# Weight pieces that begin with the kind the last one ended with, and low parts three pieces ahead, in a two-layer hybrid decoder trunk

## The chip, the cores and the metric

One core of one Trainium2 chip runs the whole computation. The metric is the device time of one execution in microseconds; a run's time is that of the slowest core, and here there is one. Engines are named as the profile names them: PE is TensorE (PEld its weight loads), DVE VectorE, ACT ScalarE, POOL GpSimd, SP SyncE, whose queue issues the weight loads.

## The reference

Two layers act on x, 256 positions by 2048 features, in float32. Cut to what matters:

```python
for l in range(DEPTH):
    h = rmsnorm(x, norm_mix_g[l])
    z = h @ w_in[l]                 # q | k | v | u | gates, 6656 columns
    y_attn = sliding_window_attention(q, k, v, q_norm_g[l], k_norm_g[l], attn_sinks[l])
    y_ssm = gelu(s5_ssm(u, ...))    # a diagonal complex state, scanned over the positions
    y_ssm = y_ssm * sigmoid(y_ssm @ ssm_glu_w[l] + ssm_glu_b[l])
    merged = g_attn * (y_attn @ w_attn_branch[l]) + g_ssm * (y_ssm @ w_ssm_branch[l])
    x = x + merged @ w_out[l]
    h2 = rmsnorm(x, norm_ffn_g[l])
    gu = h2 @ w_ffn_in[l]
    x = x + (silu(gu[..., :D_FF]) * gu[..., D_FF:]) @ w_ffn_out[l]
```

Nearly all arithmetic is in the products with weights.

## The kernel before

**Products in parts.** The activations and the weights are each split into a high part, rounded to TensorE's fp32r type, and a low part, what the rounding left. A product is high x high + low activation x high weight + high activation x low weight. The activations of one k tile (128 features) stand as [high | low], 2 x 256 columns, so a high weight tile takes one matmul of 512 columns and a low weight tile one of 256.

**Pieces.** Weights come in pieces of up to 4 k tiles by 256 output features, 512 KB each, some 880 in all, in one planned order (`want`, line 207, and the loops behind it). A slab of 256 output features takes 4 pieces where k is 2048, 2 where it is 1024 and 3 or 4 in the feed-forward output. Class `Weights` (lines 50 to 133) carries a piece through three steps, with 4 buffers each for raw pieces, high parts and low parts. `load` issues the DMA on SP's queue, `high` casts the raw piece to its high part on ScalarE (line 106), and `low` subtracts that from the raw piece on VectorE (line 121), into the low part. `low(n)` calls `high(n)` first. TensorE's loop calls `get(i)` for each piece, and `get` asks ahead:

```python
def get(self, i):
    self.high(i + 3)
    self.low(i + 2)
    self.load(i + 2 + self.LOADS)
    return self.ready.pop(i)
```

**The product loop.** `products` (line 274) takes each piece's 8 matmuls with high weights and then its 8 with low weights (lines 285 to 295: 4 k tiles, 2 tiles of 128 features), into one accumulator of two PSUM banks, of which there are 2 (`acc`). Low weights add into the second half of each bank. A few pieces aren't "wide": the first slab of the first layer takes three matmuls of 256 columns per tile, in one mixed order (line 303); so does the very last slab (line 323). The pair of slabs at line 1028 takes its pieces in turns.

**The order of everything else.** Each engine works through its instructions in the order in which the program issues them (`manual_schedule`, line 171). After each piece's matmuls `ck.tick()` (line 305) issues the jobs that are due at that piece: evictions of the slab before, a scan step, a stage of attention. `later(n, f)` sets a job n ticks ahead, `stages` runs a generator's stages one tick after the other, and `at` counts ticks from the layer's start. Jobs of a tick go in the order in which they were asked for. So the issue order is `get(i)`, matmuls of piece i, jobs of tick i, `get(i+1)`, and so on.

**A layer's order.** u, k, v and q projections; the attention gate (ga) projections; attention's output projection (ab); the SSM gate (gs) projections; GLU; the SSM's output projection (sb); the product with w_out; then the feed-forward stage in three parts, gate and up slabs (fg, fu) and output slabs (fo). Beside these:

- The scan (lines 759 to 769) is spread over the ticks up to number 110 of the layer, one or two steps a tick: products at line 766 and additions at 769, all on VectorE. Behind its last step `channels` (line 947) has its output matmuls (ys, line 963).
- Attention (lines 832 to 888) has eight head pairs, `attend(j)`, four ticks apart, the last a tick less. In one stage ScalarE takes the exponentials (line 862), VectorE adds the denominators and takes the reciprocal (lines 864 and 865), and ScalarE scales four score tiles with it (line 869); two ticks later TensorE transposes them (line 876), and a tick on makes the output y, which `split` turns into high and low parts of `ya`.
- `normed` (line 799) scales q and k: squares on ScalarE, sums on TensorE (line 806), logarithm and exponential on ScalarE (lines 369 and 370), the rest on VectorE (373 to 375).
- `evict_gs` (line 941) is issued one tick behind its slab: ScalarE copies half of the accumulator, VectorE adds the other (line 344) and multiplies by the norm (943), ScalarE takes two sigmoids (363).
- `evict_u` (line 717) has a multiplication on VectorE (719) and eight small copies, four on ScalarE (731) and four on VectorE (729).
- `coefficients` (line 562) runs on VectorE in slices of five steps a tick at the first layer's start.

Of the kernel before, what the change touches and what calls it, by code (L numbers as in the profile page):

```python
# [49 lines left out]
class Weights:  # L50
# [76 lines left out]
            self.n_low += 1  # L127

    def get(self, i):
        self.high(i + 3)  # L130
        self.low(i + 2)
        self.load(i + 2 + self.LOADS)
        return self.ready.pop(i)


# [32 lines left out]
def build(ctx, tc, a, out):  # L168
    nc = tc.nc
    v, s, g, pe = nc.vector, nc.scalar, nc.gpsimd, nc.tensor  # L170
# [12 lines left out]
    def nm(x):  # L183
        uid[0] += 1
        return f"{x}_{uid[0]}"
# [80 lines left out]
    for k, base in ((0, 0), (1, -P), (2, 0)):  # L266
# [4 lines left out]
        else:  # L271
            g.affine_select(out=nd, in_=nd, compare_op=ALU.is_gt, fill=MASKED, base=0, pattern=[[1, P]], channel_multiplier=-1)

    def products(key, rhs, wide):


        ps = accp.tile([P, 2, 512], F32, name=nm("acc"), tag="acc", bufs=2)
        pieces = plan[key]
        k = 0
        for i in pieces:  # L280
            hi, lo, m = W.get(i)
            last = i == pieces[-1]
            if wide:

                for lo_part in range(2):
                    for j in range(m):
                        x = rhs(k + j)
                        for t in range(2):
                            f = slice(t * P, t * P + P)
                            if lo_part:  # L290
                                o, w, r = ps[:, t, T:], lo[:, j, f], x[:, 0, :]
                            else:
                                o, w, r = ps[:, t, :], hi[:, j, f], x.rearrange("p a t -> p (a t)")
                            start = k + j == 0 and not lo_part
                            pe.matmul(o, w, r, start=start, stop=last and j == m - 1 and lo_part == 1, skip_group_check=True)  # L295
            else:
                for j in range(m):
                    x = rhs(k + j)
                    for t in range(2):
                        wh, wl = (w[:, j, t * P : t * P + P] for w in (hi, lo))  # L300
                        for n, (w, r) in enumerate(((wh, 0), (wh, 1), (wl, 0))):
                            start, stop = k + j + n == 0, last and j == m - 1 and n == 2
                            pe.matmul(ps[:, t, :T], w, x[:, r, :], start=start, stop=stop, skip_group_check=True)
            k += m
            ck.tick()
            yield ps

    def slab(key, rhs, wide):
        for ps in products(key, rhs, wide):
            pass  # L310
        return ps
# [14 lines left out]
    def pair(keys, rhs, wide, evict):  # L326

        gens = [products(key, rhs, wide) for key in keys]
        for _ in plan[keys[0]][:-1]:
            for gen in gens:  # L330
                next(gen)
        for i, gen in enumerate(gens):
            evict(i, next(gen))
# [43 lines left out]
    class Norm:  # L377
# [42 lines left out]
        def rhs(self, k):  # L420
            return self.h[:, k, :, :]
# [760 lines left out]
```

## Time and profile before

| | |
|---|---|
| median of 3 runs | 2632.5 us (2630.88 to 2633.15) |
| profiled execution, its own time | 2632.42 us |
| its span, first to last instruction | 2630.5 us |
| mean granted TensorE clock | 0.994 |
| instructions | 40564 |
| TensorE busy | 99% of the span |
| VectorE busy | 73% |
| ScalarE busy | 48% |
| HBM read, mean over the span | 471 MB, 181 GB/s with what is written |

The profile gives, for one execution, the busy time of each engine, groups of instructions by line, waits (who waited for whom, as inferred from semaphores) and the chain of work that ended last. In a timeline row stand the start in us, the time from the first start to the last end, the engine, the line, the operation, output tiles <- input tiles, the shape and the count of like instructions merged; a bracket shows idle time of the engine before it and what ended it. A row `x8` of matmuls spans eight that overlap each other, so the distance of starts is the better measure of their pace. Rows cut by the edge of a query's window count only what lies in it.

### The profile page before, as it was taken

The page shows a single profiled execution, that of the slowest core. Times are in us where ns is not written, and L with a number is a line of the kernel's source. Part 1 is how long each engine was busy: PE and PEld are TensorE (multiplying, and loading weights), DVE is VectorE, ACT ScalarE, POOL GpSimd, SP SyncE. Part 2 cuts the span into 40 slices and gives each one's busy share as a digit, 9 for nine tenths or more (in the row PEclk, how much of TensorE's full clock was granted, in tenths as well). Part 3 has the DMA queues.
Part 4 walks back from the last instruction along what each step waited for, and adds up shares of the span by engine and source line. Part 5 has one row for each costly group of instructions (what it writes and reads, how often), then busy time and mean ns, then how long its engine had stood idle before and what let it go on. Part 6 is the DMA issues. An engine that isn't in the chain of part 4 may idle for free.

```text
span 2630.5 us, 40564 instructions
## 1 busy us (share of the span) xinstructions
PE 2591.1 (99%) x15716; PEld 2259.7 (86%) x15716; DVE 1932.4 (73%) x3648; ACT 1267.8 (48%) x1725; POOL 29.0 (1%) x34
## 2 busy tenths in 40 slices
PE   7999899999999999999999999999999999999999
PEld 6878788888888888888888788888888888888888
DVE  8889997866765666566677999887666656665664
ACT  5666545544443444334455675465544434443442
POOL 2000000000000000000000000000000000000000
PEclk9999999999999999999999999999999999999999
DMA  6544455666655565566664445556656556655655
GB/s 203 169 129 144 145 170 164 200 209 194 203 172 191 190 189 179 192 199 187 199 201 160 141 149 170 178 173 211 213 185 187 183 199 188 190 186 187 188 180 172
DMA packets 139825, 477.85 MB, mean 182 GB/s; under 512 B 14960, under 2 KB 25456, under 8 KB 139632
## 3 DMA queue, kind: packets, MB, share of 16 engines
q1 hardware_dynamic: 139488, 475.06, 56.4%
q8 instruction: 123, 2.02, 0.3%
q14 instruction: 70, 0.57, 0.1%
q10 hardware_dynamic: 144, 0.20, 0.0%
HBM read 471.01 MB, written 4.19 MB: 181 GB/s over the span
## 4 chain that ended last, share of the span: by engine, by line
PE 81%; DVE 14%; ACT 3%; issue 1%; DMA 0%; SPq 0%; ACTq 0%; DVEq 0%
PE acc L295 79%; DVE wlo L121 5%; DVE S L769 3%; DVE sc L766 2%; ACT whi L106 1%; DVE wh L344 1%; DVE scs L855 1%; PE v L746 1%; PE ys L963 1%; ACT scs L869 1%; DVE ga L896 0%; DVE ga L916 0%; DMA w<-in_w_in 0%; PE acc L323 0%; PE bt L672 0%
## 5 line engine op out<-in xcount | busy, mean ns | idle before, releaser
L106 ACT CAST whi<-w 128x1024 fp32r<-128x1024 f32 (+1 forms) x881 | 910.6, 1047 | 769.6 <-PE acc L295 606.4
L121 DVE TENSOR_TENSOR wlo<-w,whi 128x1024 fp32r<-128x1024 f32 (+1 forms) x881 | 1061.4, 1219 | 221.2 <-ACT whi L106 220.2
L295 PE MATMUL acc<-h,whi 128*128 128x512 f32 x4448 | 1128.6, 396 | 0.8 <-DVE wh L344 0.8
L295 PEld LDWEIGHTS acc<-h,whi 128*128 128x128 f32 x4448 | 802.3, 189 | 156.8 <-issue 9.4
L295 PEld LDWEIGHTS acc<-h,wlo 128*128 128x128 f32 x4448 | 606.1, 190 | 53.5 <-DVE wlo L121 10.9
L295 PE MATMUL acc<-h,wlo 128*128 128x256 f32 x4448 | 621.8, 283 | 5.3 <-DVE wlo L121 5.3
L295 PE MATMUL acc<-hid,whi 128*128 128x512 f32 x1384 | 346.6, 392 | 0.0
L295 PEld LDWEIGHTS acc<-hid,whi 128*128 128x128 f32 x1384 | 248.9, 189 | 44.5
L337 DVE TENSOR_REDUCE j<-acc 128x512 f32<-128x1024 f32 x88 | 107.8, 1225 | 134.4 <-PE acc L295 134.4
L295 PEld LDWEIGHTS acc<-hid,wlo 128*128 128x128 f32 x1384 | 188.8, 190 | 13.5
L295 PE MATMUL acc<-hid,wlo 128*128 128x256 f32 x1384 | 193.0, 282 | 0.0
L1102 DVE TENSOR_TENSOR xn<-xn,acc 128x512 f32<-128x512 f32 x47 | 32.3, 688 | 173.5 <-PE acc L295 173.5
L769 DVE TENSOR_TENSOR S<-S,sc 128x32 f32<-128x32 f32 x1016 | 153.5, 222 | 0.0
L295 PE MATMUL acc<-mg,whi 128*128 128x512 f32 x512 | 128.2, 392 | 0.0
L766 DVE TENSOR_TENSOR sc<-scan_c,S 128x64 f32<-128x64 f32 x508 | 115.6, 269 | 0.0
L295 PEld LDWEIGHTS acc<-mg,whi 128*128 128x128 f32 x512 | 92.1, 189 | 16.5
L295 PE MATMUL acc<-yg,whi 128*128 128x512 f32 x384 | 96.2, 392 | 0.0
L295 PEld LDWEIGHTS acc<-yg,whi 128*128 128x128 f32 x384 | 69.1, 189 | 12.3
L295 PE MATMUL acc<-ya,whi 128*128 128x512 f32 x256 | 68.5, 410 | 10.0 <-DVE ya L161 6.0
L295 PEld LDWEIGHTS acc<-mg,wlo 128*128 128x128 f32 x512 | 69.8, 190 | 5.0
L351 ACT CAST hid<-j 128x512 fp32r<-128x512 f32 x44 | 27.4, 623 | 96.9 <-DVE j L1072 96.9
L295 PE MATMUL acc<-mg,wlo 128*128 128x256 f32 x512 | 71.4, 282 | 0.0
(238 smaller groups left out, 1500.7 us busy)
## 6 DMA issues: line engine op xcount, KB each, us to landing
w<-in_w_fi SPq DMA_DIRECT2D x352, 512.0 KB, 4.3
w<-in_w_in SPq DMA_DIRECT2D x207, 512.0 KB, 3.7
w<-in_w_fo SPq DMA_DIRECT2D x176, 512.0 KB, 4.4
w<-in_w_out SPq DMA_DIRECT2D x64, 512.0 KB, 4.4
w<-in_w_ab SPq DMA_DIRECT2D x32, 512.0 KB, 3.5
w<-in_w_sb SPq DMA_DIRECT2D x32, 512.0 KB, 4.1
w<-in_w_glu SPq DMA_DIRECT2D x16, 512.0 KB, 3.8
x<-in_x SPq DMA_DIRECT2D x8, 256.0 KB, 5.8
```

Source lines behind the costliest of these rows:

```text
L106: self.nc.scalar.copy(part[0][:, f, :], w[:, f, :])
L121: self.nc.vector.tensor_sub(lo[:, f, :], w[:, f, :], hi[:, f, :].bitcast(F32))
L295: pe.matmul(o, w, r, start=start, stop=last and j == m - 1 and lo_part == 1, skip_group_check=True)
L337: v.tensor_reduce(t, ps.rearrange("p s (a t) -> p s t a", a=2), axis=AX.X, op=ALU.add)
L344: v.tensor_add(t, t, ps[:, :, :T])
L351: s.copy(hi, src)
L746: pe.matmul(pss[r][:, c0 : c0 + P], bt[ri][o : o + 64, 2 * q4 + i, :], ur[o : o + 64, 2 * q4 + i, :], start=True, stop=True)
L766: v.tensor_mul(pr, scan_c[:, l, :, :, f], S[:, :, f, c - 1].unsqueeze(1).to_broadcast([P, 2, 2, 16]))
L769: v.tensor_add(S[:, :, f, c], S[:, :, f, c], pr[:, :, r, :])
L855: v.tensor_tensor_reduce(scs[b][:, f, :], scs[b][:, f, :], pv[:, f, :], 1.0, sk[:, b : b + 1], ALU.add, ALU.max, accum_out=mx[:, b, n : n ...
L869: s.activation(z, z, AF.Copy, scale=rd[:, b, n : n + 1])
L1102: v.tensor_add(t, t, ps[:, :, :T])
```

## The change

`get` asks for low parts three pieces ahead, with their casts, and for loads seven ahead of the piece in place of six. In `products` one flag, `at_low`, is kept over all pieces: a piece begins with the kind of weights that the flag names, and the flag is turned between its halves. The first matmul of a slab has the start flag whichever kind it is, the last the stop flag. Behind a piece that isn't wide the flag names low weights.

```diff
     def get(self, i):
-        self.high(i + 3)
-        self.low(i + 2)
-        self.load(i + 2 + self.LOADS)
+        self.low(i + 3)
+        self.load(i + 3 + self.LOADS)
         return self.ready.pop(i)
...
+    at_low = [False]
+
     def products(key, rhs, wide):
...
-                for lo_part in range(2):
+                for half in range(2):
+                    if half:
+                        at_low[0] = not at_low[0]
+                    lo_part = at_low[0]
                     for j in range(m):
                         x = rhs(k + j)
                         for t in range(2):
...
-                            start = k + j == 0 and not lo_part
-                            pe.matmul(o, w, r, start=start, stop=last and j == m - 1 and lo_part == 1, skip_group_check=True)
+                            start = k + j + half == 0
+                            pe.matmul(o, w, r, start=start, stop=last and j == m - 1 and half == 1, skip_group_check=True)
             else:
+                at_low[0] = True
                 for j in range(m):
```

## Rows read from the trace of the kernel before

**Rows 1.** The page's head and its busy times by engine.

```profile
span 2630.5 us, 40564 instructions
...
PE 2591.1 (99%) x15716; PEld 2259.7 (86%) x15716; DVE 1932.4 (73%) x3648; ACT 1267.8 (48%) x1725; POOL 29.0 (1%) x34
```

**Rows 2.** The chain that ended last, by line: 427 to 1370 us, then 290 to 400.

```profile
by line: PE acc L295 99.3%; PE bt L672 0.4%; PE ms L417 0.2%; PE k L683 0.1%
...
by line: DVE wlo L121 34.6%; DVE S L769 22.6%; DVE sc L766 17.8%; DVE ga L916 5.0%; ACT whi L106 4.6%; DVE wh L344 4.4%; DMA w<-in_w_in 3.1%; DVE gs L943 2.5%; DVE gs L344 2.2%; issue 2.1%; PE ys L963 0.6%; ACT gs L363 0.5%; ACTq L106 0.1%;
```

**Rows 3.** Busy time by stretch: bounds and length in us, then each engine, clock, DMA.

```profile
157.00:290.00 133.00, 125.49 (x760) 103.40 (x759) 128.54 (x534) 86.87 (x200) 3.63 (x2) 0.96 0.44 137
290.00:400.00 110.00, 103.33 (x590) 87.57 (x588) 109.35 (x433) 51.90 (x70) 0.00 (x0) 1.00 0.52 164
1440.00:1590.00 150.00, 145.39 (x895) 121.66 (x894) 145.78 (x558) 99.33 (x214) 3.63 (x2) 0.99 0.47 148
...
427.00:1370.00 943.00, 943.00 (x5534) 830.37 (x5533) 641.75 (x696) 430.58 (x503) 4.47 (x3) 1.00 0.60 193
1745.00:2630.00 885.00, 881.91 (x5074) 776.83 (x5072) 573.21 (x598) 375.37 (x411) 0.00 (x0) 1.00 0.59 190
```

**Rows 4.** Waits of VectorE, 157 to 290 us: total us, times, longest.

```profile
DVE wlo L121 <- ACT whi L106: 0.8, 2, 0.6
```

**Rows 5.** Waits of TensorE over the whole span: total us, times, longest.

```profile
PE acc L295 <- DVE ya L161: 6.0, 2, 3.8
...
PE ys L963 <- DVE S L769: 2.1, 1, 2.1
```

**Rows 6.** Timeline of TensorE in the feed-forward stage; the last two from narrower windows.

```profile
1005.84 2.00 PE L295 MATMUL acc<-h,whi 128*128 128x512 f32 x8
1007.68 1.11 PE L295 MATMUL acc<-h,wlo 128*128 128x256 f32 x8
1008.64 2.00 PE L295 MATMUL acc<-h,whi 128*128 128x512 f32 x8
...
1007.00 0.84 PE L295 MATMUL acc<-h,whi 128*128 128x512 f32 x3
...
1007.92 0.88 PE L295 MATMUL acc<-h,wlo 128*128 128x256 f32 x6
```

**Rows 7.** Timeline at one gs eviction, VectorE and ScalarE.

```profile
351.94 1.22 DVE L121 TENSOR_TENSOR wlo<-w,whi 128x1024 fp32r<-128x1024 f32 x1
352.07 0.91 ACT L363 ACTIVATE gs<-gs,params 128x256 f32<-128x256 f32 x2 [2.90 <-DVE gs L943]
352.88 1.98 ACT L106 CAST whi<-w 128x1024 fp32r<-128x1024 f32 x2
```

**Rows 8.** Timeline at one head pair's reciprocal, second layer, VectorE, then ScalarE.

```profile
1509.09 1.22 DVE L121 TENSOR_TENSOR wlo<-w,whi 128x1024 fp32r<-128x1024 f32 x1
...
1508.96 1.50 ACT L869 ACTIVATE scs<-scs,sm 128x128 f32<-128x128 f32 x4 [1.85 <-DVE sm L865]
1510.36 1.03 ACT L106 CAST whi<-w 128x1024 fp32r<-128x1024 f32 x1
```

**Rows 9.** Timeline at one query norm, second layer, VectorE, then ScalarE.

```profile
1437.30 1.22 DVE L121 TENSOR_TENSOR wlo<-w,whi 128x1024 fp32r<-128x1024 f32 x1
...
1439.63 1.99 ACT L106 CAST whi<-w 128x1024 fp32r<-128x1024 f32 x2
```

**Rows 10.** Timeline where the GLU begins in the first layer.

```profile
436.05 2.94 ACT L106 CAST whi<-w 128x1024 fp32r<-128x1024 f32 x3
...
438.50 1.78 PE L295 MATMUL acc<-yg,whi 128*128 128x512 f32 x7
```

**Rows 11.** Timeline of the first layer's start: TensorE, VectorE, ScalarE.

```profile
24.81 0.58 PE L303 MATMUL acc<-h,wlo 128*128 128x256 f32 x1 [6.25 <-DVE wlo L121]
...
52.43 1.23 DVE L121 TENSOR_TENSOR wlo<-w,whi 128x1024 fp32r<-128x1024 f32 x1
...
52.89 2.95 ACT L106 CAST whi<-w 128x1024 fp32r<-128x1024 f32 x3
```

## The prediction

> **What bounds the kernel now.** The page's busy line comes first: TensorE is busy for 2591.1 of 2630.5 us [rows 1], so at first sight anything that TensorE does in fewer nanoseconds is gained. That is an average over stages, so the chain of waits is read by stretch next. From 427 to 1370 us it is 99.3% TensorE matmuls. From 290 to 400 us it is nearly all VectorE: low-part subtractions 34.6%, the two scan lines 22.6% and 17.8% [rows 2]. Third, busy time by stretch [rows 3]: VectorE is busy for 128.54 of 133 us (157 to 290), 109.35 of 110 (290 to 400) and 145.78 of 150 (1440 to 1590), but for 641.75 of 943 in the long stretch between and 573.21 of 885 in the last. So two regions, one in each layer, from the query projections through attention to the end of the scan, are set by VectorE; elsewhere TensorE is alone. Fourth, what VectorE waits for: in the first of these stretches, a cast of ScalarE's for 0.8 us in all [rows 4]. It is never starved, so what is added to its path moves the region's end. Two waits of TensorE show that the ends hang on VectorE: 2.1 us for the scan's last addition before the output matmuls, 6.0 us in two waits for the last attention output's low part [rows 5].
>
> **Part 1, the order of kinds.** A piece is 8 matmuls of 512 columns (high weights) and 8 of 256 (low). In the feed-forward stage the high run lasts from 1005.84 to 1007.68 us, 1.84 us. Its last three start at 1007.00, so three take 0.68 us, 0.227 each; the first five take 1.16, 0.232 each. At the later rate eight would be 1.813, so entering high weights costs 0.027 us. The low run shows no such cost: 0.24 us for its first two matmuls, 0.72 for the other six, 0.12 each [rows 6]. Now every piece enters both kinds; after the change two pieces share one entry into each. That saves 0.027 us in two pieces, or at worst 0.02 if the entry into low is a little faster than the print shows: 0.012 a piece on the whole. It counts only where TensorE is alone, (943 + 885) us at 2.80 us a piece (1005.84 to 1008.64), 653 pieces: **-7.9 us** (bounds -6.5 and -9). In the VectorE regions it is worth nothing.
>
> The Trainium skill, page "TensorE: Matmul & The Clock Gate", section "Back-to-back issue gap", gives the gap as N/2.4 + 2.5 ns, by the column count alone. By that the order of kinds would save nothing and the sum below would end 8 us higher. The rows decide for the smaller time: their gap falls from 232 to 227 ns within one run of equal N.
>
> **Part 2, low parts three pieces ahead.** No instruction is added; 881 casts, subtractions and loads stay. What moves is each subtraction on VectorE's queue: by one piece, ahead of one tick's jobs. That is also right behind its own cast, which stays three ahead on ScalarE. Before, the cast of piece i+3 and the subtraction of i+2 were issued together, so the cast had a piece to finish. Now VectorE stops at the subtraction until the cast is done; behind it on its queue stand the scan step, the evictions and everything of the next tick. Where ScalarE's cast itself stands behind an operation that waits for VectorE's job of the same tick, the round trip lies open. I price each from the rows as cast end minus the time at which VectorE is through with that tick (where it now starts its subtraction); both move together if VectorE is late.
>
> - Gate eviction (gs), in the scan: VectorE is free at 351.94; ScalarE's sigmoids run from 352.07 and the first cast from 352.88, ending at 353.93, as one is 1.05 us [rows 7]: 2.0 us. Evictions of four slabs fall before the scan's last step: 8.0 us a layer.
> - Attention: VectorE is free at 1509.09 behind its reciprocal; ScalarE scales four tiles with it (1508.96, 1.50 us), then casts, to 1511.39 [rows 8]: 2.3 us. Eight head pairs a layer, of which the last is issued a tick earlier and has other work behind it: seven, 16.1 us a layer. The covering work was the 1.22 us subtraction of the piece before and a scan step; these are not lost, they are done earlier, when VectorE was not yet short.
> - Query norm, once a layer as the region begins: VectorE is free at 1437.30 and the cast ends at 1440.68, since ScalarE waits for TensorE's sums there [rows 9]: 3.4 us at most, 0 if the slack of the projections hides it. I take 2, as VectorE hardly waits afterwards.
> - After the scan, the same round trips until the GLU: three casts run from 436.05 to 438.99 behind such a sigmoid, and TensorE starts the GLU's first piece at 438.50 [rows 10], so a subtraction that must follow its cast there comes about when it is needed. Between 0 and 4 us a layer (two round trips); I take 2.
> - First layer's start: the 6.25 us wait at 24.81 us [rows 11] goes, as that subtraction is now issued ahead of the first slice of coefficients. VectorE has that slice still to do before the next subtraction, so the wait comes a piece later and is shorter. Against it, each of three u evictions opens a gap, free at 52.43, cast to 53.94 [rows 11]: 1.5 us, 4.5 in all, plus one more subtraction of 1.22 ahead. Between -3 and +6; I take +3.
>
> Three moves I cost at nothing. The loads: each is still issued right behind the subtraction that frees its buffer, on SP's queue, which carries nothing else that is urgent. The buffers: where a piece begins low, its high part is read 0.95 us later, so the cast that takes its place waits so much longer; in the feed-forward stage over 300 us of VectorE's 943 are idle, which cover it. The start flag moves to whichever half comes first and adds no matmul. If that cover goes, the third rival's price applies.
>
> **Sum.** Per layer 8.0 + 16.1 + 2 + 2 = 28.1 us, two layers 56.2, the start 3, less 7.9: +51.3 us. The profiled execution took 2632.4 us, 1.9 around its span, and stands 0.1 under the median of 2632.5, so the forecast is **2684 us**. With attention half hidden (-16), the start and both small terms at their best (-6, -8), or these at their worst (+10), its own range is 2660 to 2700.
>
> **Rivals.** (a) *Not slower*: the round trips fit in slack, since each subtraction is a whole piece earlier. For it: TensorE's 99%. It would need VectorE to find 2 us free in every four pieces of attention and scan; it has 0.65 in 110 us [rows 3]. The point that decides is the last scan step of the first layer: if TensorE doesn't wait longer there than the 2.1 us of now, only -7.9 and up to -3 are left: 2622 to 2627, or up to 2632 if a few trips show. (b) *Only the scan's end pays*: in attention TensorE has its own extra matmuls, and in the second layer it has 4.6 us idle of 150 against VectorE's 4.2, so the engines are close and slack may swallow most of the 16.1. Then 16 + 4 + 3 - 8 = +15 us: 2647 (2637 to 2660). Against: the last attention output sits on VectorE's own queue, so its delay adds whatever TensorE's slack is. (c) *The feed-forward stage stalls too*: if the later release of high buffers or the sigmoid's round trip costs 0.5 us in every eighth piece or more, 653/8 x 0.5 = 41 us come on top: 2725. Against: VectorE's idle third. (d) *The order of kinds saves nothing*, the high entry cost being tied to something else, such as the switch of piece: 2692. The Trainium skill's gap rule, above, is this case. The rows against it: the cost decays inside the run.
>
> **Numbers.** Forecast 0.52, (a) 0.20, (b) 0.18, (c) 0.05, (d) 0.05. A measurement can tell about 0.2%, 5 us, from no change. Of (a) 0.16 lies below 2627 and 0.04 within the bound; 0.02 of (b) also lies within. So faster 0.16, same 0.06, slower 0.78. The range runs from 2630, to hold (b), to 2705, to hold the unknown bounds and (d); it leaves out most of (a) and all of (c).
>
> **What would show it.** Right: VectorE's waits for casts rise by some 2 us at each gs eviction and each head pair in the two regions, TensorE waits for low parts or the scan there, matmul runs of 16 have one slow entry, a pair of pieces drops from 5.60 to some 5.575 us in the feed-forward stage. Wrong: VectorE's busy share in 290 to 400 us stays at 99% and the region's end doesn't move; or the feed-forward pieces get longer.

## The result, and the profile after

The changed kernel takes **2735.4 us** (median of 4 runs, 2734.4 to 2738.6) against 2632.6 for the kernel before on the same chip: a ratio of 1.039, 95% interval 1.038 to 1.041, or 102.9 us more. The direction was forecast, the size was not: 2684 us with a range of 2630 to 2705. The profiled execution took 2735.25 us, with a span of 2733.2.

First the page's head, its busy times, its chain by engine and its costliest group of VectorE, to be held against [rows 1]:

```profile
span 2733.2 us, 40610 instructions
...
PE 2613.4 (96%) x15716; PEld 2272.2 (83%) x15716; DVE 1944.4 (71%) x3648; ACT 1258.8 (46%) x1725; POOL 29.8 (1%) x34
...
PE 72%; DVE 19%; ACT 5%; issue 3%; DMA 0%; SPq 0%; ACTq 0%; DVEq 0%
...
L121 DVE TENSOR_TENSOR wlo<-w,whi 128x1024 fp32r<-128x1024 f32 (+1 forms) x881 | 1072.0, 1221 | 701.3 <-ACT whi L106 700.8
```

The work is the same: as many matmuls, and busy times that have moved by some per cent at most. What has grown is idle time: VectorE now stands 700.8 us before its subtractions, waiting for casts (220.2 before). That number is not the loss. Some 470 us of it lie in the feed-forward stages (651 to 1381 and 1993 to 2730 us), where VectorE has time to spare and nobody waits for it. The page cannot tell harmful waits from harmless ones; for that the two traces are set side by side, by the start of the same piece's first matmul:

| piece, and what ends there | before, us | after, us | after minus before | gained or lost on the way |
|---|---|---|---|---|
| 28, start of the first layer | 109.8 | 118.9 | +9.1 | +9.1 |
| 76, query norm and most of attention | 294.1 | 321.6 | +27.5 | +18.4 |
| 116, gate evictions, end of the scan | 427.3 | 461.6 | +34.3 | +6.8 |
| 156, last gate slab, GLU, SSM projection (sb), part of w_out | 539.1 | 595.6 | +56.5 | +22.2 |
| 436, nearly all of the feed-forward stage | 1327.1 | 1381.2 | +54.1 | -2.4 |
| 468, start of the second layer | 1428.9 | 1485.1 | +56.2 | +2.1 |
| 516, query norm and attention | 1596.1 | 1671.2 | +75.1 | +18.9 |
| 556, gate evictions, end of the scan | 1720.3 | 1803.2 | +82.9 | +7.8 |
| 596, last gate slab, GLU, sb, part of w_out | 1832.1 | 1937.1 | +105.0 | +22.1 |
| 872, nearly all of the feed-forward stage | 2603.9 | 2706.6 | +102.7 | -2.3 |

Most of the table is as forecast: attention with the query norm was put at 18.1 a layer, the gate evictions at 8. The surprise stands in the two lines with 22, pieces 116 to 156, for which the forecast had one term: 2 us until the GLU begins. The GLU's first piece, 120, starts at 438.5 us before and at 478.8 after, so 6.0 us are lost up to there (5.9 in the second layer) and 16.2 behind it, for which there was no term at all.

Next, the busy time by stretch, as in [rows 3], with the stretches shifted to where the same work now lies (attention, end of scan, GLU and sb of the first layer; attention of the second; the feed-forward stage):

```profile
172.00:318.00 146.00, 126.20 (x729) 101.63 (x728) 126.29 (x534) 84.55 (x196) 3.62 (x2) 0.93 0.40 123
318.00:437.00 119.00, 105.05 (x629) 90.45 (x631) 110.61 (x433) 51.37 (x70) 0.00 (x0) 0.99 0.52 155
...
461.00:540.00 79.00, 67.48 (x359) 58.10 (x357) 50.76 (x61) 41.20 (x60) 0.00 (x0) 0.94 0.47 148
...
1521.00:1668.00 147.00, 132.79 (x787) 106.88 (x787) 127.23 (x505) 90.72 (x205) 3.62 (x2) 0.97 0.43 133
600.00:1375.00 775.00, 774.80 (x4585) 685.12 (x4584) 516.24 (x539) 330.30 (x367) 4.46 (x3) 1.00 0.62 192
```

In attention and scan VectorE was idle before for 4.5 of 133 us, 0.7 of 110 and 4.2 of 150 [rows 3]; now it is for 19.7 of 146, 8.4 of 119 and 19.8 of 147. In 461 to 540 us **no engine is full**: TensorE 67.5 of 79, VectorE 50.8, ScalarE 41.2. Two engines that wait for each other in turn look like this. These 79 us hold some 22 pieces. Before, a stretch from the same piece on had TensorE full, and some 28 pieces in 78 us:

```profile
427.00:505.00 78.00, 78.00 (x449) 68.62 (x448) 66.79 (x81) 49.70 (x72) 0.00 (x0) 1.00 0.62 195
```

VectorE's waits for casts, by window: 318 to 437, then 461 to 540, then 1521 to 1668 us (total, times, longest):

```profile
DVE wlo L121 <- ACT whi L106: 7.9, 5, 1.9
...
DVE wlo L121 <- ACT whi L106: 24.9, 15, 1.9
...
DVE wlo L121 <- ACT whi L106: 16.1, 7, 2.6
```

The first, four waits of 1.91 at gate evictions and one of 0.30, and the third are the forecast's 8.0 and 16.1, where before there was 0.2 us and none; attention in the first layer, 172 to 318 us, has 16.0, where it had 0.8 [rows 4]. The second is 15 waits of 1.66 us, where the forecast had looked at two and hidden half of their time. Over all of pieces 116 to 156 there are 24, of 39.0 us.

One gate eviction in the timeline (VectorE, ScalarE, TensorE), to be read against [rows 7]:

```profile
407.54 0.69 DVE L949 TENSOR_TENSOR gs<-gs,rms 128x512 f32<-128x512 f32 x1
408.27 0.91 ACT L369 ACTIVATE gs<-gs,params 128x256 f32<-128x256 f32 x2 [8.87 <-DVE gs L949]
409.08 3.87 ACT L106 CAST whi<-w 128x1024 fp32r<-128x1024 f32 x4
410.14 1.22 DVE L121 TENSOR_TENSOR wlo<-w,whi 128x1024 fp32r<-128x1024 f32 x1 [1.91 <-ACT whi L106]
...
411.42 1.21 PE L300 MATMUL acc<-h,wlo 128*128 128x256 f32 x8 [2.41 <-DVE wlo L121]
```

VectorE is through at 408.23 and stands until the two sigmoids and the first of the casts are done. Before, the subtraction at that place belonged to a piece whose cast was long finished, and ran beside the sigmoids. Here TensorE waits as well, at the end of the chain. One head pair of attention, against [rows 8]:

```profile
1588.46 1.49 ACT L875 ACTIVATE scs<-scs,sm 128x128 f32<-128x128 f32 x4 [1.84 <-DVE sm L871]
...
1589.86 1.98 ACT L106 CAST whi<-w 128x1024 fp32r<-128x1024 f32 x2
...
1590.92 1.23 DVE L121 TENSOR_TENSOR wlo<-w,whi 128x1024 fp32r<-128x1024 f32 x1 [2.25 <-ACT whi L106]
```

This was priced at 2.3 us and is 2.25.

Now the part that was missed. One slab of the GLU in the after kernel, VectorE first, then ScalarE:

```profile
495.88 0.68 DVE L350 TENSOR_TENSOR glu<-glu,acc 128x512 f32<-128x512 f32 x1
498.48 1.23 DVE L121 TENSOR_TENSOR wlo<-w,whi 128x1024 fp32r<-128x1024 f32 x1 [1.91 <-ACT whi L106]
499.62 0.68 DVE L1017 SCALAR_TENSOR_TENSOR glu<-glu,y 128x512 f32<-128x512 f32 x1
501.99 1.23 DVE L121 TENSOR_TENSOR wlo<-w,whi 128x1024 fp32r<-128x1024 f32 x1 [1.69 <-ACT whi L106]
503.13 0.69 DVE L160 TENSOR_TENSOR yg<-glu,yg 128x512 fp32r<-128x512 f32 x1
503.74 0.68 DVE L350 TENSOR_TENSOR glu<-glu,acc 128x512 f32<-128x512 f32 x1
...
496.60 0.91 ACT L369 ACTIVATE glu<-glu,params 128x256 f32<-128x256 f32 x2 [2.00 <-DVE glu L350]
497.41 1.03 ACT L106 CAST whi<-w 128x1024 fp32r<-128x1024 f32 x1
500.39 0.62 ACT L357 CAST yg<-glu 128x512 fp32r<-128x512 f32 x1 [1.95 <-DVE glu L1017]
500.92 1.04 ACT L106 CAST whi<-w 128x1024 fp32r<-128x1024 f32 x1
```

Follow one turn. VectorE adds (495.88), ScalarE takes sigmoids and casts (to 498.44), VectorE subtracts and only then multiplies (to 500.30), ScalarE rounds and casts (to 501.96), VectorE subtracts, makes yg and adds again at 503.74. But for one copy of 0.58 us the two never work at the same time. A turn is 7.86 us (503.74 - 495.88) for the two pieces of a slab, and TensorE needs only 5.57 for them. Before, the subtraction ran beside the sigmoid:

```profile
451.10 1.22 DVE L121 TENSOR_TENSOR wlo<-w,whi 128x1024 fp32r<-128x1024 f32 x1
451.21 0.91 ACT L363 ACTIVATE glu<-glu,params 128x256 f32<-128x256 f32 x2 [0.75 <-DVE glu L344]
...
452.23 0.69 DVE L1011 SCALAR_TENSOR_TENSOR glu<-glu,y 128x512 f32<-128x512 f32 x1
```

How TensorE pays for it, in its own timeline from the GLU's first piece to the first pieces of sb:

```profile
478.76 2.08 PE L300 MATMUL acc<-yg,wlo 128*128 128x256 f32 x8 [4.51 <-DVE wlo L121]
480.63 5.80 PE L300 MATMUL acc<-yg,whi 128*128 128x512 f32 x16
486.26 2.06 PE L300 MATMUL acc<-yg,wlo 128*128 128x256 f32 x16
488.16 3.82 PE L300 MATMUL acc<-yg,whi 128*128 128x512 f32 x16
...
512.33 3.58 PE L300 MATMUL acc<-yg,whi 128*128 128x512 f32 x8 [4.79 <-DVE glu L350]
```

and what released the last of these rows, on VectorE:

```profile
511.59 0.68 DVE L350 TENSOR_TENSOR glu<-glu,acc 128x512 f32<-128x512 f32 x1
```

Inside the GLU it hardly waits: pieces made ready ahead cover the lag. The lag is settled in one wait of 4.79 us, before sb's second piece: this takes the accumulator of the GLU's last slab, which VectorE has finished reading only at 512.27. The 4.51 before it is a debt of the same kind, from the gelu units ahead of the GLU, where VectorE's subtractions follow each other by 4.07 us (467.09 to 471.16) for pieces of 2.8, and from a gate slab. Behind both waits the matmuls begin at half pace: 16 high ones take 5.80 us and not 3.82, 8 low ones 2.08 and not 1.11, 8 high ones 3.58 and not 2.00 [rows 6]. That is 1.98 + 0.97 + 1.58 = 4.5 us, and the granted clock says why (0.50, which is 1.2 GHz, until about 485, then 1.00, which is 2.4 GHz, again). How much of it is in the 22.2 was not tested: VectorE ended the second wait, and a TensorE at full clock would have stood there for longer.

```profile
478.70:481.50 2.80, 2.74 (x11) 2.55 (x12) 2.80 (x5) 2.07 (x3) 0.00 (x0) 0.50 0.63 178
...
486.00:490.00 4.00, 4.00 (x26) 3.59 (x25) 1.86 (x2) 1.84 (x4) 0.00 (x0) 1.00 0.61 194
```

Last, the feed-forward stage, where only the order of kinds should count:

```profile
1059.26 3.82 PE L300 MATMUL acc<-h,whi 128*128 128x512 f32 x16
1062.92 2.08 PE L300 MATMUL acc<-h,wlo 128*128 128x256 f32 x16
1064.83 3.82 PE L300 MATMUL acc<-h,whi 128*128 128x512 f32 x16
```

A high run of 16 lasts 3.66 us (1062.92 - 1059.26), where two runs of 8 took 3.68 [rows 6]. A pair of pieces is 5.57 us (1064.83 - 1059.26), against 2 x 2.80 before; in the median over the feed-forward stages 5.567 against 5.587. The forecast had 5.575.

### The profile page after: what moved, and what is told of

It is laid out like the page before. It is cut to its first block, busy times and chain, and to the rows that moved or that the text cites. A ratio compares the mean times of both kernels' runs of the same rounds, so it can differ in the third digit from the quotient of the medians.

```text
span 2733.2 us, 40610 instructions
## 1 busy us (share of the span) xinstructions
PE 2613.4 (96%) x15716; PEld 2272.2 (83%) x15716; DVE 1944.4 (71%) x3648; ACT 1258.8 (46%) x1725; POOL 29.8 (1%) x34
## 4 chain that ended last, share of the span: by engine, by line
PE 72%; DVE 19%; ACT 5%; issue 3%; DMA 0%; SPq 0%; ACTq 0%; DVEq 0%
PE acc L300 69%; DVE wlo L121 7%; DVE S L775 3%; ACT whi L106 3%; DVE sc L772 2%; ACT scs L875 1%; DVE scs L861 1%; DVE wh L350 1%; PE v L752 1%; PE ys L969 1%; DVE sb L1031 0%; DVE sb L1030 0%; DVE mg L160 0%; DVE sb L350 0%; PE acc L329 0%
## 5 line engine op out<-in xcount | busy, mean ns | idle before, releaser
L121 DVE TENSOR_TENSOR wlo<-w,whi 128x1024 fp32r<-128x1024 f32 (+1 forms) x881 | 1072.0, 1221 | 701.3 <-ACT whi L106 700.8
L300 PE MATMUL acc<-h,whi 128*128 128x512 f32 x4448 | 1085.9, 395 | 0.0
L300 PEld LDWEIGHTS acc<-h,whi 128*128 128x128 f32 x4448 | 822.6, 190 | 168.3 <-issue 9.0
L300 PEld LDWEIGHTS acc<-h,wlo 128*128 128x128 f32 x4448 | 576.4, 192 | 59.2 <-DVE wlo L121 30.9
L300 PE MATMUL acc<-h,wlo 128*128 128x256 f32 x4448 | 595.3, 285 | 31.2 <-DVE wlo L121 27.2
L300 PE MATMUL acc<-hid,whi 128*128 128x512 f32 x1384 | 330.2, 391 | 0.0
L300 PEld LDWEIGHTS acc<-hid,wlo 128*128 128x128 f32 x1384 | 177.8, 191 | 6.7
L300 PE MATMUL acc<-hid,wlo 128*128 128x256 f32 x1384 | 180.4, 283 | 0.0
L300 PEld LDWEIGHTS acc<-yg,whi 128*128 128x128 f32 x384 | 75.5, 202 | 25.7 <-DVE glu L350 10.4
L369 ACT ACTIVATE sg<-j 128x512 f32<-128x512 f32 x44 | 27.8, 633 | 139.3 <-DVE j L1067 139.3
L300 PE MATMUL acc<-yg,wlo 128*128 128x256 f32 x384 | 54.6, 291 | 16.4 <-DVE wlo L121 9.0
```

Of the source, the lines that this page charges most:

```text
L121: self.nc.vector.tensor_sub(lo[:, f, :], w[:, f, :], hi[:, f, :].bitcast(F32))
L369: s.activation(o, i, AF.Sigmoid, **kw)
```

## The experiments

Three theories go in. **R**: the time is lost in round trips, since a subtraction now stands right behind its own cast on the other engine. **K**: the new order of kinds itself costs something. **J**: the subtraction now stands ahead of a tick's jobs and takes their place on VectorE, whatever the cast does. Edits are shown against the after kernel, in `get` where nothing else is said; all runs are compared with the kernel before, run on the same chip.

**1. The order of kinds alone.** `at_low` stays, `get` is that of before.

```diff
-        self.low(i + 3)
-        self.load(i + 3 + self.LOADS)
+        self.high(i + 3)
+        self.low(i + 2)
+        self.load(i + 2 + self.LOADS)
```

> The order of kinds alone, with the asking ahead of before (casts three, low parts two, loads six). Theory R (round trip: the 103 us come from each subtraction standing right behind its own cast, so that VectorE stops wherever that cast stands behind a ScalarE operation that waits for VectorE): 2621 to 2632 us, since the loss is gone, the feed-forward pieces keep their 10 ns each, and in the VectorE regions low-first pieces may wait a little. Theory K (the order of kinds is what costs, as half of the pieces need their low part 1.84 us earlier and hold their high part longer): some 2735 us. Theory J (the subtraction now stands ahead of a tick's jobs, so that evictions and scan steps come later, whether or not it waits for a cast): 2621 to 2632, as R.

Measured: 2625.7 us (10 runs) against 2631.1, a ratio of 0.9979 (0.9970 to 0.9989): 5.4 us faster, with 2.9 to 7.9 as its interval. K is out. By piece starts this kernel gains 2.9 us on the kernel before between pieces 156 and 436 and 2.8 between 596 and 872, some 0.010 a piece; at the end of the first scan it stands 0.3 us ahead, after a loss of 1.2 at the start. Its median is the lowest of this study, below both kernels.

**2. Low parts three ahead alone.** The after kernel's `get`, the kinds in the order of before (with the flags of before, not shown).

```diff
-                for half in range(2):
-                    if half:
-                        at_low[0] = not at_low[0]
-                    lo_part = at_low[0]
+                for lo_part in range(2):
```

> Low parts three pieces ahead alone, each piece high first as before. R: 2725 to 2745 us, the loss of the whole change without its 8 us gain, perhaps a little less as no piece begins low. K: 2625 to 2640. J: 2725 to 2745. VectorE's wait for casts, 220 us before and 701 us after, should be near 700 by R and J.

Measured: 2741.8 us, ratio 1.042 (1.040 to 1.044): 110.7 us over the kernel before beside it. That is all of the loss, and 7.8 us more than with the order of kinds, which by run 1 saves 5.4. The two parts of the change add, as far as the intervals tell. VectorE's waits for casts are 654.1 us, not far from the 700 expected.

**3. The cast one tick sooner.** The subtraction stays three ahead, in its new place ahead of the tick's jobs, but its cast is issued at the end of the piece before, in front of that tick's jobs.

```diff
+            W.high(i + 4)
             k += m
             ck.tick()
```

> The whole change, and the cast of piece i+4 is issued behind piece i's matmuls and ahead of tick i's jobs, in place of behind them. The subtraction stays where the change put it, ahead of the next tick's jobs, but its cast no longer stands behind ScalarE's operations of the tick. R: below 2650 us, near 2620 to 2640, and VectorE's wait for casts in the regions falls back. K: 2700 us or more. J: 2700 us or more, as the subtraction is as early as in the changed kernel.

Measured: 2639.1 us, ratio 1.0026 (1.0015 to 1.0037). So it is 7.9 us over the kernel before beside it, and 95 of the 103 us are gone, although every subtraction stands where the change put it. J is out and R stands: it is the order of cast and subtraction across the two queues. The loads, seven ahead here too, are no part of it. VectorE's waits for casts fell back in the regions, as R asked: from piece 44 to 116 (174 to 435 us here, 182 to 462 in the after kernel) to 0.8 from 27.8 us, from 116 to 156 to 8.0 from 39.0. The stretch from piece 116 to 156 loses nothing now (0.4 us shorter than before, against 22.2 longer). Yet its total of waits, most of it in the feed-forward stage, is

```profile
DVE wlo L121 <- ACT whi L106: 522.5, 434, 5.1
```

which is worth keeping in mind: 75% of the waits of the after kernel, with almost none of the loss. The 13 us that remain over run 1 come mostly at the start (+1.8 by piece 28), between there and piece 116 (+5.7), and in the second layer between pieces 468 and 556 (+7.3). VectorE's waits for ScalarE's copy out of an accumulator (`whole`, names `wh`) are 39.3 us in all, 22.5 in run 1. That casts now stand ahead of ScalarE's own jobs would fit; it was not tested. A fifth high buffer, with casts four ahead and subtractions three, was not tried either.

**4 to 6. Where it is lost.** Each takes run 1 and asks three ahead in one stretch alone.

```diff
-        self.low(i + 3)
-        self.load(i + 3 + self.LOADS)
+        n = 3 if 110 <= i % 440 < 176 else 2
+        self.high(i + 3)
+        self.low(i + n)
+        self.load(i + n + self.LOADS)
```

> As the run of the order of kinds alone, but pieces 110 to 175 of each layer (the end of the gs slabs, the GLU, the sb and the w_out slabs) ask for low parts three ahead. The trace of the changed kernel lost 22 us a layer between its pieces 116 and 148. R: 40 to 48 us over the run of the order alone, with TensorE waiting for low parts and accumulators in the GLU. The prediction's term of 2 us a layer for this stretch: 4 us over. K: no difference from the run of the order alone.

Measured (GLU, sb, w_out): 2670.5 us, ratio 1.015 (1.013 to 1.017), **44.7 us over run 1**. This alone is what lies behind the scans, where the forecast had 2 x 2. The waits of TensorE that it opens are those of the after kernel: 4.50 us before the GLU's first low part, 4.79 before sb's second piece, some 0.8 in each sb slab.

The next one has `n = 3 if i < 40 else 2`, the first layer's start:

> The order of kinds, with low parts three ahead for the first 40 pieces alone. The changed kernel stood 9.1 us behind at piece 28, the run of the order alone 1.2. R: 7 to 9 us over the run of the order alone (2625.7), so 2633 to 2635, from the first slice of coefficients' successor waits and the u evictions. The prediction's term: 3 us. If the start's first wait were the whole matter, faster by up to 3.

Measured: 2632.6 us, ratio 1.0005 (0.9996 to 1.0014): 0.8 us over the kernel before beside it, so 6.2 over run 1 (0.8 + 5.4). The start costs about 6, the upper bound, where 3 had been taken from a range of -3 to 6.

The third has `n = 3 if 40 <= i % 440 < 110 else 2`, attention and scan in both layers:

> The order of kinds, with low parts three ahead for pieces 40 to 109 of each layer alone: attention, ab and the scan. R: 48 to 56 us over the run of the order alone (2674 to 2682), as the changed kernel lost 25 us in the first layer's stretch and 27 in the second's, and the run of the order alone nothing; the prediction's terms (16.1 + 8.0 + 2 a layer) give 52. By the rival that only the scan's end pays: 16 to 20 us over, 2642 to 2646. The three ranges together (44.7 measured, 8 and 52) should give back the 110 us between the changed kernel and the run of the order alone.

Measured: 2678.4 us, ratio 1.018 (1.016 to 1.019): 46.6 over the kernel before beside it, 52.0 over run 1. This is R's number and not that of rival (b), which had some 16 to 20 here. The three together make 44.7 + 6.2 + 52.0 = 102.9 of the 108.3 us (102.9 + 5.4) between run 1 and the changed kernel; some 5 us are left to places between the ranges, or to a range's edge (the second layer's start, pieces 440 to 479, lies in none).

The same starts of pieces as above, each minus the kernel before, show the three parts in their places:

| piece | 28 | 76 | 116 | 156 | 436 | 468 | 516 | 556 | 596 | 872 |
|---|---|---|---|---|---|---|---|---|---|---|
| after | +9.1 | +27.5 | +34.3 | +56.5 | +54.1 | +56.2 | +75.1 | +82.9 | +105.0 | +102.7 |
| run 1, order alone | +1.2 | -0.1 | -0.3 | -0.5 | -3.4 | -3.6 | -5.2 | -3.9 | -4.0 | -6.8 |
| run 3, cast sooner | +3.0 | +4.9 | +7.2 | +6.8 | +3.9 | +3.7 | +6.8 | +10.7 | +10.3 | +7.5 |
| run 4, GLU | +1.2 | -0.1 | -0.3 | +21.6 | +18.7 | +18.5 | +16.6 | +18.3 | +40.2 | +37.4 |
| run 6, scan | +1.5 | +16.9 | +25.7 | +25.6 | +22.7 | +22.5 | +41.1 | +50.1 | +50.0 | +47.2 |

Losses stay: none of the slack of the feed-forward stage gives anything back, because TensorE is full there and goes at its own pace.

**7. One piece.** `n = 3 if i == 0 else 2`: can the 6.25 us wait of [rows 11] be had for nothing?

> The order of kinds, with low parts three ahead for the first piece alone: the subtraction of piece 3 is issued ahead of the first slice of coefficients. R: the 6.25 us wait for it goes, and comes back in part a piece later; 2621 to 2626 us, as VectorE's chain through the coefficients is as long as before. If the wait were simply removed: 2619 us.

Measured: 2628.8 us (11 runs), ratio 0.9989 (0.9980 to 0.9998). A miss: 3.0 us under the kernel before, so no gain over run 1 with its 5.4, and by piece starts none either (-6.8 at piece 872 in both, although the profiled execution, at 2625.6 us, is the fastest of the eleven). TensorE's longest wait for a low part in the first 100 us moves one piece on and is no shorter: 6.9 us, in run 1 it is 6.3. The forecast had said that "the wait comes a piece later and is shorter". VectorE's first slice of coefficients stands in the way wherever the subtraction is put.

**8. Two entries in a piece.** The kernel before, each piece in four parts, high, low, high, low, of 2 k tiles each.

```diff
-                for lo_part in range(2):
-                    for j in range(m):
+                for part in range(4):
+                    lo_part = part % 2
+                    for j in range(m // 2 * (part // 2), m // 2 * (part // 2) + m // 2):
```

> The kernel before, with each piece taken in four parts, high, low, high, low, two k tiles each: two entries into each kind for a piece in place of one. If entering high weights costs 0.02 to 0.027 us, as the rows were read, 653 pieces outside the VectorE regions give +13 to +18 us: 2644 to 2649. If the gap hangs on the column count alone, or on the switch of piece: no difference, 2631.

Measured: 2641.2 us, ratio 1.0036 (1.0024 to 1.0049), 9.3 us slower; less than the 13 to 18 expected, clearly more than nothing. Its TensorE timeline:

```profile
1003.27 1.09 PE L296 MATMUL acc<-h,whi 128*128 128x512 f32 x4
1004.20 0.63 PE L296 MATMUL acc<-h,wlo 128*128 128x256 f32 x4
...
1006.08 1.09 PE L296 MATMUL acc<-h,whi 128*128 128x512 f32 x4
```

A piece is 2.81 us (1006.08 - 1003.27), where it had been 2.80. More entries cost more, with the column counts unchanged. Rival (d) had the order save nothing; runs 1 and 8 say otherwise, from both sides. The rule of the Trainium skill that stood beside it (page "TensorE: Matmul & The Clock Gate", section "Back-to-back issue gap": a gap by the column count alone, given there for an isolated matmul) does not hold to that accuracy here: in the feed-forward stage of the kernel before the median distances of starts in a high run of eight are 233, 236, 228, 232, 231, 227, 227, 227 ns.

## Why the prediction was right or wrong

Against the forecast's terms, in us (by piece starts, first and second layer):

| term | forecast | measured |
|---|---|---|
| order of kinds, both layers | -7.9 | -5.4 (run 1) |
| query norm and attention, a layer | 2 + 16.1 | 18.4 and 18.9 |
| gate evictions to the scan's end, a layer | 8.0 | 6.8 and 7.8 |
| after the scan until the GLU, a layer | 2 (0 to 4) | 6.0 and 5.9 |
| GLU and sb, a layer | none | 16.2 and 16.2 |
| start of the first layer | 3 (-3 to 6) | 9.1 (run 5 alone: 6.2) |
| start of the second layer | not named | 2.1 |

**The mechanism was right.** "VectorE stops at the subtraction until the cast is done": run 3 puts the cast ahead by one tick, changes nothing else, and takes away 95 of 103 us. The single prices were good to a tenth: 2.0 forecast and 1.91 measured for a gate eviction, 2.3 and 2.25 for a head pair.

**The step that failed** is "After the scan, the same round trips until the GLU ... Between 0 and 4 us a layer (two round trips); I take 2". Two things are wrong in it. At the place that it names, the GLU's first piece, the subtraction does not come "about when it is needed": TensorE waits 4.51 us for it, and 6.0 us are lost up to there. And it ends there, as if the matter were settled: the GLU and sb slabs behind it stand in the sum at nothing, and up to piece 156 there are twenty more waits (33.3 us) and a loss of 16.2. They had been judged by "elsewhere TensorE is alone", from VectorE's 641.75 busy of 943 us. In the stretch that matters VectorE was busy for 66.79 of 78 and ScalarE for 49.70 of 78; neither is a bound alone. But 66.79 + 49.70 = 116.5 is more than 78: the two fitted only since they ran beside each other. Taken in turns, as the change makes them in every slab of the GLU, they are the bound. A turn of 7.86 us for two pieces against 5.57, over the four slabs, is 9.2 us, and pieces 120 to 130 lost 10.0; the sb slabs behind, up to 148, lost 6.3, about 1 each. To count waits, as for attention, would not have given it: 24 waits of 39.0 us a layer are more than the 22.2 that were lost.

**The start** was mis-sized, 3 for 6 to 9. The gap at u evictions was seen; that the removed wait would return a piece later in full was not (run 7), nor was the 5.64 us instruction below.

**The order of kinds** came out at the figure per piece that had been read (0.010 measured, 0.012 forecast), and its sum below the bounds of -6.5 to -9 in the median, though the interval of the run (2.9 to 7.9) reaches into them; 1.2 us went at the start. The forecast's own range is added up wrongly: its terms make 2654 to 2694, where it says 2660 to 2700. The measured time lies outside either.

**The rivals.** (a) fell, but not by the sign that was to decide it: TensorE's longest wait for the scan before the first layer's output matmuls is 1.6 us, no longer than the 2.1 of before [rows 5], and yet the stretch up to there grew by 34.3. That the delay would show in that one wait was itself not right. It shows in earlier ones (the whole span, both layers):

```profile
PE acc L300 <- DVE wlo L121: 36.2, 17, 4.9
PE pt L882 <- ACT scs L875: 15.4, 11, 2.2
...
PE acc L300 <- DVE ya L160: 9.1, 2, 5.0
...
PE ys L969 <- DVE S L775: 2.7, 4, 1.6
```

(b) fell with run 6. (c) fell: feed-forward pieces got shorter, with VectorE waiting some 470 us in them for nothing that matters. (d) fell with runs 1 and 8. The range held (b), which was wrong, and not a larger loss of the same kind as the forecast's own, which is what came.

## What to carry to other kernels

Where two in-order engines hand work to each other, keep the consumer one job group behind its producer: asking for both at the same distance opens a round trip at every job that crosses the other way, here some 1 to 2.3 us each and 103 us in all, though not one instruction was added. To cost such a move, don't ask which engine is full. Follow one turn between the two engines, and hold it against the time that TensorE needs for the same pieces: 7.86 us against 5.57 in the GLU. The sum of the two engines' busy times does not settle it: it is over the stretch's length around the GLU (116.5 of 78 us before), but in the feed-forward stage, too (514.57 + 336.61 us of 775, from 600 to 1375 us before), and that lost nothing. There a slab has three or four pieces, in the GLU and sb two; whether that makes the difference was not tested. The total of a wait says little: 522 us of it went with 7.9 us over the kernel before in run 3, and 39 us with 22 around the GLU.

## What had not been expected of the hardware

**A small instruction of VectorE that took 5.64 us.** At the first layer's start, VectorE and GpSimd in the after kernel:

```profile
26.16 1.21 DVE L121 TENSOR_TENSOR wlo<-w,whi 128x1024 fp32r<-128x1024 f32 x1
27.29 5.64 DVE L461 TENSOR_SCALAR cw<-cw 128x64 f32<-128x64 f32 x1
...
28.45 3.54 POOL L655 MEMSET pw<- 128x2048 f32 x2
31.94 0.94 POOL L684 MEMSET k<- 128x1024 f32 x1
```

Operations of the same size take 0.2 us later in the run, and the four ahead of this one, beside other work of GpSimd's, 1.3 each. This one ends at 32.93 and GpSimd's work at 32.88, so it seems to have stood until GpSimd was through; and the next subtraction is queued behind it. It was not tested by an edit. Nor does it come every time: it is there in runs 2 and 3 (5.65 us each), but in the profiled execution of run 5, which asks the same of these pieces as the after kernel, the operation was short:

```profile
26.58 1.26 DVE L463 TENSOR_SCALAR cw<-cw 128x64 f32<-128x64 f32 x1
```

That execution stands 4.7 us behind at piece 28 and not 9.1, the same 4.4 us less. In run 3, with the long one, it is only 3.0, so the start has more to it. The Trainium skill, page "SBUF — State Buffer", section "SBUF: two separate sides", says that whichever of VectorE (in some of its operations) and GpSimd starts first holds a shared port pair for its whole instruction while the other is fully blocked. The rows agree as far as VectorE stood while GpSimd worked, but through three of GpSimd's instructions; which operations of VectorE it concerns, no run here shows.

**TensorE's clock after a wait.** The forecast priced waits at their length. Behind the waits of 4.51 and 4.79 us the granted clock was 0.50, and the matmuls behind the first took 2.95 us longer than others, those behind the second 1.58. Whether that came on top of the waits or only shortened the next one, no run separates. Over the whole execution the mean granted clock is 0.988, against 0.994 before and 0.998 in run 1.

**Entering a kind of weights has no single price.** Two pieces that share their entries are 0.020 us shorter (5.587 to 5.567, medians), for one entry less into each kind. In run 8 one entry more into each kind, in runs half as long, costs 0.013 a piece (3.7 us over pieces 156 to 436). What makes the difference was not tested.
